# Gate products of the last stage as two 64-row halves of TensorE's array, added when PSUM is read

## Chip, cores and metric

The kernel runs on one NeuronCore of a Trainium2 chip, as one launch. The metric is the device time of that launch in microseconds (us). All inputs and the output lie in HBM, and everything is float32. The profile is of one execution; its trace has every instruction with its start and duration.

## What is computed

The reference is one layer of a hybrid decoder on 512 tokens of 2048 channels. The change lies in its last step, a gated input embedding ahead of the final norm:

```python
n3 = rms_norm(h, norm_ple[i])
h = h + jax.nn.sigmoid(n3 @ w_ple_gate[i]) * (p[i] @ w_ple_proj[i])
return rms_norm(h, norm_final)
```

`n3 @ w_ple_gate` is a product of 512x2048 with 2048x2048. What stands ahead of it (pooling mixer, gated DeltaNet, a mixture of 32 experts) is computed as before, and so is `p @ w_ple_proj`, which is ready when the last stage begins.

## The kernel before

Tokens lie on partitions in NT = 4 groups of P = 128, called t; the 2048 channels that are summed over are KD = 16 groups of 128, called k. Float32 products are made to float32 accuracy from a rounded part (hi, of type float32r) and a rest (lo): `mm3` (line 97) issues hi*hi, hi*lo and lo*hi into one PSUM bank, at lines 99, 100 and 101. Each is a matmul with a weight load of its own. The scheduler of the framework may order the three as it likes.

A PSUM bank holds 128x512 float32. There are eight: `bank("mm")` and `bank("dl")` hand out four each, in turn, and a bank is handed out again once its reader is done.

`last_norm` (four calls, 512 channels each) transposes h and writes it as `xh` and `xl`, 128 channels by 512 tokens for each k. These are the stationary operands of the last stage: 128 channels (the array's rows) by 128 tokens (its columns).

`tail` (line 1532) is the last stage. It walks over the 2048 output channels in five blocks: three of 512, one of 256 (starting at channel 1536) and a last one of 256.

- Blocks 0 to 3 share a loop. For every k and every t one `mm3` adds to the bank of t. The banks of the four t are taken from "mm" in blocks 0 and 2 and from "dl" in blocks 1 and 3.
- `gate_weights` (line 1523) hands out the gate's weights, split into hi (a ScalarE copy, line 94) and lo (a VectorE subtraction, line 95) in pieces of 128x1024, four buffers each.
- After a block `finish` runs for each t: a tanh on ScalarE out of PSUM (line 1549), two operations on VectorE (lines 1551 and 1554), a sum of squares on ScalarE (line 1556) and a product with the final gain on GpSimd (line 1557). Its buffer `th3` exists twice.
- Block 4 goes t by t instead, with one "dl" bank for each, and ends with the final norm of that t and the store.

Two places ahead of the last stage already use parts of TensorE's array. The router (line 919) multiplies with 36 columns of weights and puts the product of k into PSUM partitions from 64 * (k % 2) on, so that even and odd k use different halves of the array's columns. The experts (lines 1138 and 1197) put two experts of 64 slots side by side in the same way, in pairs of matmuls to partitions 0 to 63 and 64 to 127 of one bank. Both use all 128 rows and plain float32, and in the trace a plain float32 product stands as two matmuls.

The order on each engine in this stage is set by the framework's scheduler, not by hand.

Of the kernel before, what the change touches and what calls it, by code (L numbers as in the profile page):

```python
# [13 lines left out]
AF = mybir.ActivationFunctionType  # L14
OP = mybir.AluOpType
# [4 lines left out]
NT = T // P  # L20
D = 2048
KD = D // P
# [40 lines left out]
class Layer:  # L63
# [33 lines left out]
    def mm3(self, ps, whi, wlo, xhi, xlo, start, stop):  # L97
        mm = self.nc.tensor.matmul
        mm(ps, whi, xhi, start=start, stop=False)  # L99
        mm(ps, whi, xlo, start=False, stop=False)  # L100
        mm(ps, wlo, xhi, start=False, stop=stop)  # L101


    def identity(self):
# [1427 lines left out]
    def tail(self, pp):  # L1532
        nc, a, ss, xh, xl = self.nc, self.a, self.ss3, self.xh, self.xl
        gain, _ = self.take("gain", (D,))
        self.fill_stream(1000)
        nc.sync.dma_start(gain, bass.AP(tensor=a["norm_final"].tensor, offset=a["norm_final"].offset,
                                        ap=[[0, P], [1, D]]))
        m = pp.tile([P, NT], F32, name="ms3", bufs=1)
        nc.vector.tensor_reduce(m, ss, axis=AX.X, op=OP.add)
        nc.vector.tensor_scalar(m, m, 1.0 / D, EPS, op0=OP.mult, op1=OP.add)  # L1540
        hr = pp.tile([P, NT], F32, name="hr3", bufs=1)
        self.rsqrt(pp, hr, m, NT)
        nc.vector.tensor_scalar(hr, hr, 0.5, None, op0=OP.mult)
        ss4 = pp.tile([P, NT, 5], F32, name="ss4", bufs=1)

        def finish(t, c0, w, i, ps):
            cs = slice(c0, c0 + w)
            th = pp.tile([P, T], F32, name="th3", bufs=2)
            nc.scalar.activation(th[:, 0:w], ps[:, 0:w], AF.Tanh, scale=hr[:, t:t + 1])
            o = c0 % T  # L1550
            nc.vector.scalar_tensor_tensor(th[:, 0:w], th[:, 0:w], 1.0, self.pj[t, c0 // T][:, o:o + w],
                                           op0=OP.add, op1=OP.mult)
            d = self.h[:, t, cs]
            nc.vector.scalar_tensor_tensor(d, th[:, 0:w], 0.5, d, op0=OP.mult, op1=OP.add)
            j = self.p_sq.tile([P, T], BF16, name="sqj", bufs=1)
            nc.scalar.activation(j[:, 0:w], d, AF.Square, accum_out=ss4[:, t, i:i + 1])
            nc.gpsimd.tensor_tensor(d, d, gain[:, cs], op=OP.mult)

        for i, (c0, w) in enumerate(((0, 512), (512, 512), (1024, 512), (1536, 256))):
            tag = "dl" if i % 2 else "mm"  # L1560
            ps = [self.bank(tag) for _ in range(NT)]
            k = 0
            while k < KD:
                for hi, lo in self.gate_weights(w):
                    for j in range(1024 // w):
                        for t in range(NT):
                            s = slice(t * P, (t + 1) * P)
                            self.mm3(ps[t][:, 0:w], xh[k][:, s], xl[k][:, s], hi[:, j, :], lo[:, j, :],
                                     start=k == 0, stop=k == KD - 1)
                        k += 1  # L1570
            for t in range(NT):
                finish(t, c0, w, i, ps[t])
        c0, w = 1792, 256
        ws = [part for _ in range(2) for part in self.gate_weights(w)]
        for t in range(NT):
            ps = self.bank("dl")
            s = slice(t * P, (t + 1) * P)
            for k in range(KD):
                hi, lo = ws[k // 4]
                self.mm3(ps[:, 0:w], xh[k][:, s], xl[k][:, s], hi[:, k % 4, :], lo[:, k % 4, :],  # L1580
                         start=k == 0, stop=k == KD - 1)
            finish(t, c0, w, 4, ps)
            m = pp.tile([P, 1], F32, name="ms4", bufs=2)
            nc.vector.tensor_reduce(m, ss4[:, t, :], axis=AX.X, op=OP.add)
            nc.vector.tensor_scalar(m, m, 1.0 / D, EPS, op0=OP.mult, op1=OP.add)
            r = pp.tile([P, 1], F32, name="r4", bufs=2)
            self.rsqrt(pp, r, m, 1)
            ht = self.h[:, t, :]
            nc.vector.tensor_scalar(ht[:, 0:D // 2], ht[:, 0:D // 2], r, None, op0=OP.mult)
            nc.scalar.activation(ht[:, D // 2:], ht[:, D // 2:], AF.Copy, scale=r)  # L1590
            nc.sync.dma_start(a["out"][0, t * P:(t + 1) * P, :], ht)
# [115 lines left out]
```

## Time and profile before

| | us |
|---|---|
| median of 2 runs | 2620.73 (2619.27 to 2622.2) |
| the profiled execution's own time | 2616.97 |
| its span, first to last instruction | 2614.9 |
| TensorE (PE) busy | 2511.0, 96% of the span |
| VectorE (DVE) busy | 1148.9 |
| ScalarE (ACT) busy | 776.7 |
| mean granted clock of TensorE | 0.992 of 2.4 GHz |

The profiled execution lies 3.76 us under the median. 2.1 us of its time lie outside the span. The last stage is its last 190 us or so, from 2424 us on. PE counts matmuls and PEld weight loads, which are instructions of their own and may run beside a matmul. A matmul's duration holds the time until its results are written, so that durations of neighbours overlap: what one costs in a row of many is the distance between starts.

### The profile page before, as it was taken

What the parts mean: (1) busy time and instruction counts of PE and PEld (TensorE: products, weight loads), DVE (VectorE), ACT (ScalarE), POOL (GpSimd) and SP (SyncE); (2) the same over time, 40 slices, a digit from 0 to 9 for tenths busy, and PEclk for the clock granted to TensorE, in tenths of its full rate; (3) what the DMA queues carried; (4) which work ended last, traced back from release to release, by engine and by line L of the source; (5) the groups of instructions that cost most, each with busy time, mean ns of one, the idle gap of its engine ahead of it and who ended that gap; (6) DMA issues with size and microseconds to landing.
All of it is one profiled execution on the core that took longest, in us unless ns stands there. A gap on an engine that the chain in (4) does not pass through costs nothing. (4 is left out here: it accounts for less than half of the span.)

```text
span 2614.9 us, 30940 instructions
## 1 busy us (share of the span) xinstructions
PE 2511.0 (96%) x12358; PEld 1720.5 (66%) x12358; DVE 1148.9 (44%) x2042; ACT 776.7 (30%) x1308; POOL 83.8 (3%) x92
## 2 busy tenths in 40 slices
PE   7999999999999999999989899999999999989998
PEld 6788888887888888877754444444444444444788
DVE  6475766765222233345453343333334333315435
ACT  4233242424222222234434222223222222113323
POOL 1001110100000000000000000000000000000001
PEclk9999999999999999999989999999999999999999
DMA  5222223234333333373237799999999999977222
GB/s 153 81 79 73 79 58 94 68 97 125 97 97 97 97 97 97 97 292 126 81 138 283 324 378 416 379 422 374 422 377 421 384 421 376 401 307 278 97 97 97
DMA packets 197975, 554.16 MB, mean 212 GB/s; under 512 B 30378, under 2 KB 127043, under 8 KB 148035
## 3 DMA queue, kind: packets, MB, share of 16 engines
q1 hardware_dynamic: 194610, 543.61, 55.4%
q10 hardware_dynamic: 2640, 4.33, 0.5%
q0 software_dynamic: 576, 4.19, 0.4%
q8 instruction: 99, 1.62, 0.2%
q14 instruction: 50, 0.40, 0.0%
HBM read 545.01 MB, written 7.08 MB: 211 GB/s over the span
## 5 line engine op out<-in xcount | busy, mean ns | idle before, releaser
L1138 PE MATMUL ps_mm<-wm,xe 128*64 128x512 f32 x2048 | 454.7, 597 | 10.6 <-DMA wm<-in_w_gate_dram 5.3
L99 PE MATMUL ps_mm<-n1h,whi 128*128 128x512 f32 x1120 | 450.4, 402 | 0.9 <-ACT whi L94 0.9
L101 PE MATMUL ps_mm<-n1h,wlo 128*128 128x512 f32 x1120 | 437.3, 391 | 1.7 <-DVE wlo L95 1.6
L100 PE MATMUL ps_mm<-n1l,whi 128*128 128x512 f32 x1120 | 437.1, 390 | 0.0
L95 DVE TENSOR_TENSOR wlo<-raw,whi 128x1024 fp32r<-128x1024 f32 x206 | 254.4, 1235 | 412.5 <-ACT whi L94 401.4
L94 ACT CAST whi<-raw 128x1024 fp32r<-128x1024 f32 x206 | 216.3, 1050 | 545.1 <-PE ps_mm L100 538.9
L1138 PEld LDWEIGHTS ps_mm<-wm,xe 128*64 128x64 f32 x2048 | 141.8, 137 | 287.0 <-issue 264.1
L95 DVE TENSOR_TENSOR glo<-h,ghi 128x512 fp32r<-128x512 f32 x128 | 137.2, 1096 | 361.1 <-ACT ghi L94 352.8
L94 ACT CAST ghi<-h 128x512 fp32r<-128x512 f32 x128 | 139.6, 1134 | 425.3 <-PE ps_dl L1113 314.2
L101 PEld LDWEIGHTS ps_mm<-n1h,wlo 128*128 128x128 f32 x1120 | 210.0, 188 | 47.3 <-DVE wlo L95 2.5
L99 PEld LDWEIGHTS ps_mm<-n1h,whi 128*128 128x128 f32 x1120 | 210.8, 188 | 40.3 <-ACT whi L94 1.3
L100 PEld LDWEIGHTS ps_mm<-n1l,whi 128*128 128x128 f32 x1120 | 210.9, 188 | 38.7
L1197 PE MATMUL ps_mm<-wm,hmT 128*64 128x512 f32 x960 | 218.8, 601 | 9.0 <-DVE eidx L1353 6.9
L1221 DVE TENSOR_TENSOR h<-h,ps_dl 128x512 f32<-128x512 f32 x256 | 160.2, 682 | 98.7 <-PE ps_dl L1219 95.9
L1197 PEld LDWEIGHTS ps_mm<-wm,hmT 128*64 128x64 f32 x960 | 66.5, 137 | 135.2 <-issue 130.0
L1113 PE MATMUL ps_dl<-G,ghi 128*128 128x256 f32 x512 | 134.2, 298 | 1.9 <-DVE G L1092 0.9
L1114 PE MATMUL ps_dl<-G,glo 128*128 128x256 f32 x512 | 128.5, 288 | 5.2 <-DVE glo L95 5.2
L1113 PEld LDWEIGHTS ps_dl<-G,ghi 128*128 128x128 f32 x512 | 99.2, 194 | 42.4 <-issue 38.9
L1218 PE MATMUL ps_dl<-yhi,GT 128*128 128x512 f32 x256 | 107.8, 421 | 14.0 <-ACT xe L1120 14.0
L1114 PEld LDWEIGHTS ps_dl<-G,glo 128*128 128x128 f32 x512 | 99.2, 194 | 7.1 <-DVE glo L95 6.9
L101 PE MATMUL ps_mm<-whi,ml 128*128 128x512 f32 x256 | 100.0, 391 | 2.1 <-DVE ml L95 2.1
L1219 PE MATMUL ps_dl<-ylo,GT 128*128 128x512 f32 x256 | 100.7, 393 | 0.0
(402 smaller groups left out, 3262.4 us busy)
## 6 DMA issues: line engine op xcount, KB each, us to landing
wm<-in_w_gate_dram SPq DMA_DIRECT2D x128, 1024.0 KB, 8.7
wm<-in_w_up_dram SPq DMA_DIRECT2D x128, 1024.0 KB, 10.2
wm<-in_w_down_dram SPq DMA_DIRECT2D x128, 1024.0 KB, 9.5
raw<-in_w_in_dram SPq DMA_DIRECT2D x144, 512.0 KB, 3.7
raw<-in_w_out_dram SPq DMA_DIRECT2D x32, 512.0 KB, 3.7
wm<-in_w_ple_gate_dram SPq DMA_DIRECT2D x16, 1024.0 KB, 5.0
raw<-in_w_up_dn_dram SPq DMA_DIRECT2D x16, 512.0 KB, 3.5
raw<-in_w_up_pool_dram SPq DMA_DIRECT2D x16, 512.0 KB, 3.6
```

Of the source, the lines that this page charges most:

```text
L94: i = self.nc.scalar.copy(hi, src)
L95: return i, self.nc.vector.tensor_tensor(lo, src, hi.bitcast(F32), op=OP.subtract)
L99: mm(ps, whi, xhi, start=start, stop=False)
L100: mm(ps, whi, xlo, start=False, stop=False)
L101: mm(ps, wlo, xhi, start=False, stop=stop)
L1113: nc.tensor.matmul(p, hi[:, t, :], Gf[:, t, :], start=t == 0, stop=False)
L1114: nc.tensor.matmul(p, lo[:, t, :], Gf[:, t, :], start=False, stop=t == NT - 1)
L1138: nc.tensor.matmul(ps[64 * i:64 * i + 64, :], xe[k][:, c0 + 64 * i:c0 + 64 * i + 64], ws[i][:, j, :], start=k == 0, stop=k == KD - 1)
L1197: nc.tensor.matmul(out[cb][64 * i:64 * i + 64, :], hT[:, k, 64 * i:64 * i + 64], ws[i][:, cb * T:(cb + 1) * T], start=k == 0, stop=k == 3)
L1218: nc.tensor.matmul(pc, GT[:, s], yh, start=True, stop=False)
L1219: nc.tensor.matmul(pc, GT[:, s], yl, start=False, stop=True)
L1221: nc.vector.tensor_tensor(d, d, pc, op=OP.add)
```

## The change

A new helper `mm3_rows` takes the place of `mm3` in blocks 0 to 3. For each of the three products it issues two matmuls in place of one: the first with the upper 64 rows of both operands, the second with the lower 64. The halves go to two banks, one "mm" and one "dl", so that a block now holds all eight. `finish` begins with a ScalarE copy of the first bank into `th3` and a VectorE addition of the second; the tanh then reads `th3` in place of PSUM. Block 4 is as it was: it hands `finish` a list of one bank.

```diff
+    def mm3_rows(self, ps, whi, wlo, xhi, xlo, start, stop):
+
+        mm = self.nc.tensor.matmul
+        for w, x, first, last in ((whi, xhi, start, False), (whi, xlo, False, False), (wlo, xhi, False, stop)):
+            for i, r in enumerate((slice(0, 64), slice(64, 128))):
+                mm(ps[i], w[r], x[r], start=first, stop=last)
...
         def finish(t, c0, w, i, ps):
             cs = slice(c0, c0 + w)
             th = pp.tile([P, T], F32, name="th3", bufs=2)
-            nc.scalar.activation(th[:, 0:w], ps[:, 0:w], AF.Tanh, scale=hr[:, t:t + 1])
+            if len(ps) == 2:
+                nc.scalar.copy(th[:, 0:w], ps[0][:, 0:w])
+                nc.vector.tensor_tensor(th[:, 0:w], th[:, 0:w], ps[1][:, 0:w], op=OP.add)
+                ps = [th]
+            nc.scalar.activation(th[:, 0:w], ps[0][:, 0:w], AF.Tanh, scale=hr[:, t:t + 1])
...
         for i, (c0, w) in enumerate(((0, 512), (512, 512), (1024, 512), (1536, 256))):
-            tag = "dl" if i % 2 else "mm"
-            ps = [self.bank(tag) for _ in range(NT)]
+            ps = [[self.bank("mm"), self.bank("dl")] for _ in range(NT)]
...
-                            self.mm3(ps[t][:, 0:w], xh[k][:, s], xl[k][:, s], hi[:, j, :], lo[:, j, :],
-                                     start=k == 0, stop=k == KD - 1)
+                            self.mm3_rows([p[:, 0:w] for p in ps[t]], xh[k][:, s], xl[k][:, s], hi[:, j, :],
+                                          lo[:, j, :], start=k == 0, stop=k == KD - 1)
...
-            finish(t, c0, w, 4, ps)
+            finish(t, c0, w, 4, [ps])
```

The scheduler's order moves at the seams between blocks. TensorE where block 0 ends and block 1 begins, before: the banks of block 1 ("dl") are others than those of block 0 ("mm"). In a row stand the output, then the moving operand and the stationary one.

```order
L101 MATMUL ps_mm_17156<-whi_17361,xl_17094 128x512
L99 MATMUL ps_dl_17417<-whi_17423,xh_16908 128x512 [waits Activation_49]
L100 MATMUL ps_dl_17417<-wlo_17424,xh_16908 128x512 [waits DVE_49]
L101 MATMUL ps_dl_17417<-whi_17423,xl_16909 128x512
L99 MATMUL ps_dl_17418<-whi_17423,xh_16908 128x512 [waits PE_49]
```

The same place with the change, from the end of block 0 through t = 0 and the start of t = 1; t = 2 stands like t = 1:

```order
L108 MATMUL ps_dl_17160<-whi_17533,xl_17094 128x512
L108 MATMUL ps_mm_17621<-whi_17631,xh_16908 128x512 [waits Activation_49]
L108 MATMUL ps_dl_17622<-whi_17631,xh_16908 128x512 [waits DVE_49]
L108 MATMUL ps_mm_17621<-wlo_17632,xh_16908 128x512
L108 MATMUL ps_dl_17622<-wlo_17632,xh_16908 128x512
L108 MATMUL ps_mm_17621<-whi_17631,xl_16909 128x512
L108 MATMUL ps_dl_17622<-whi_17631,xl_16909 128x512
L108 MATMUL ps_mm_17623<-whi_17631,xh_16908 128x512 [waits Activation_49]
L108 MATMUL ps_dl_17624<-whi_17631,xh_16908 128x512 [waits DVE_49]
```

The two halves of a product now stand one behind the other, and the first of each t waits for ScalarE and its partner for VectorE. For t = 3 the three of the "mm" bank stand ahead of the three of the "dl" bank.

ScalarE at the same seam, before:

```order
L1549 ACTIVATE th3_17389<-ps_mm_17153,hr3_17138 128x512 [waits PE_49]
L1549 ACTIVATE th3_17396<-ps_mm_17154,hr3_17138 128x512 [waits PE_49]
L94 CAST whi_17509<-wm_17331 128x1024 [waits DVE_49,PE_49]
L1556 ACTIVATE sqj_17393,ss4_17152<-h_8839 128x512 [waits DVE_49]
L1549 ACTIVATE th3_17403<-ps_mm_17155,hr3_17138 128x512
```

And with the change (line 1557 is now the copy, 1560 the tanh, 1567 the sum of squares):

```order
L1557 COPY th3_17585<-ps_mm_17153 128x512 [waits PE_49]
L1560 ACTIVATE th3_17585<-th3_17585,hr3_17138 128x512 [waits DVE_49]
L1557 COPY th3_17594<-ps_mm_17155 128x512 [waits PE_49]
L1560 ACTIVATE th3_17594<-th3_17594,hr3_17138 128x512 [waits DVE_49]
L1567 ACTIVATE sqj_17591,ss4_17152<-h_8839 128x512 [waits DVE_49]
L1557 COPY th3_17603<-ps_mm_17157 128x512 [waits PE_49]
L94 CAST whi_17789<-wm_17479 128x1024 [waits PE_49,Activation_49]
L1567 ACTIVATE sqj_17600,ss4_17152<-h_8839 128x512 [waits DVE_49,Activation_49]
L1560 ACTIVATE th3_17603<-th3_17603,hr3_17138 128x512 [waits DVE_49]
L1557 COPY th3_17612<-ps_mm_17159 128x512
```

The copy that frees the first bank of t = 1 now stands behind the tanh of t = 0, which waits for an addition of VectorE; the copies of t = 2 and t = 3 stand behind sums of squares, a weight split and a tanh.

VectorE there with the change (1558 is the addition, 1562 and 1565 the two operations behind it):

```order
L1558 TENSOR_TENSOR th3_17585<-th3_17585,ps_dl_17154 128x512 [waits PE_49,Activation_49]
L1562 SCALAR_TENSOR_TENSOR th3_17585<-th3_17585,pj_15929 128x512 [waits Activation_49]
L1558 TENSOR_TENSOR th3_17594<-th3_17594,ps_dl_17156 128x512 [waits PE_49,Activation_49]
L1565 SCALAR_TENSOR_TENSOR h_8839<-th3_17585,h_8839 128x512 [waits DVE_49]
L1562 SCALAR_TENSOR_TENSOR th3_17594<-th3_17594,pj_15938 128x512 [waits Activation_49]
L1565 SCALAR_TENSOR_TENSOR h_8839<-th3_17594,h_8839 128x512 [waits DVE_49]
L1558 TENSOR_TENSOR th3_17603<-th3_17603,ps_dl_17158 128x512 [waits PE_49,Activation_49]
L95 TENSOR_TENSOR wlo_17790<-wm_17479,whi_17789 128x1024 [waits Activation_49]
L1562 SCALAR_TENSOR_TENSOR th3_17603<-th3_17603,pj_15987 128x512 [waits Activation_49]
L1558 TENSOR_TENSOR th3_17612<-th3_17612,ps_dl_17160 128x512 [waits DVE_49,PE_49,Activation_49]
```

Before, VectorE had no part in freeing a bank here; now the four additions that free the second banks are spread among the eight operations of `finish` and a weight split.

## Rows read from the trace of the kernel before

**Rows 1.** The page, busy us (share of the span) and instructions of each engine.

```profile
PE 2511.0 (96%) x12358; PEld 1720.5 (66%) x12358; DVE 1148.9 (44%) x2042; ACT 776.7 (30%) x1308; POOL 83.8 (3%) x92
```

**Rows 2.** Windows of blocks 1, 3, 4: us, busy of PE PEld DVE ACT POOL, clock, DMA.

```profile
2469.75:2514.50 44.75, 44.75 (x193) 35.97 (x192) 17.41 (x17) 13.49 (x20) 6.32 (x4) 1.00 0.29 95
...
2559.30:2581.70 22.40, 22.40 (x193) 22.35 (x193) 11.74 (x12) 8.71 (x16) 6.33 (x4) 1.00 0.15 48
2581.70:2614.90 33.20, 22.61 (x194) 22.41 (x193) 19.41 (x69) 11.86 (x28) 6.63 (x8) 0.87 0.31 127
```

**Rows 3.** Timeline inside block 0: start us, duration us, engine, line, operation.

```profile
2435.22 0.39 PE L101 MATMUL ps_mm<-whi,xl 128*128 128x512 f32 x1
2435.22 0.19 PEld L99 LDWEIGHTS ps_mm<-whi,xh 128*128 128x128 f32 x1
2435.45 0.40 PE L99 MATMUL ps_mm<-whi,xh 128*128 128x512 f32 x1
```

**Rows 4.** Timeline inside block 3, products 256 wide.

```profile
2569.97 0.28 PE L100 MATMUL ps_dl<-wlo,xh 128*128 128x256 f32 x1
2569.97 0.19 PEld L101 LDWEIGHTS ps_dl<-whi,xl 128*128 128x128 f32 x1
2570.09 0.28 PE L101 MATMUL ps_dl<-whi,xl 128*128 128x256 f32 x1
```

**Rows 5.** TensorE's timeline at 1192 and 1339 us, router products of 36 columns.

```profile
1192.11 1.05 PE L919 MATMUL ps_dl<-hT,wr 128*36 128x512 f32 x2
...
1339.29 1.06 PE L919 MATMUL ps_dl<-hT,wr 128*36 128x512 f32 x4 [0.80 <-ACT hT L917]
```

**Rows 6.** Timeline of weight loads in an expert stage, products of 64 columns.

```profile
2372.05 0.14 PEld L1197 LDWEIGHTS ps_mm<-wm,hmT 128*64 128x64 f32 x2 [0.29 <-issue]
2372.48 0.14 PEld L1197 LDWEIGHTS ps_mm<-wm,hmT 128*64 128x64 f32 x2 [0.28 <-issue]
```

**Rows 7.** The expert products of line 1197: duration ns min/median/max; a window of them.

```profile
L1197 PE MATMUL ps_mm<-wm,hmT x960: 592/592/1116, 1466.1 to 2378.1; 128*64 128x512 f32 x192
...
2371.57:2378.00 6.43, 6.43 (x30) 2.21 (x32) 1.00 1.05 387
```

**Rows 8.** Timeline at 2412.9 us, a product whose weight load nothing covers.

```profile
2412.89 0.50 PE L1218 MATMUL ps_dl<-yhi,GT 128*128 128x512 f32 x1
2413.23 0.40 PE L1219 MATMUL ps_dl<-ylo,GT 128*128 128x512 f32 x1
...
2412.89 0.19 PEld L1218 LDWEIGHTS ps_dl<-yhi,GT 128*128 128x128 f32 x1 [0.24 <-DVE xl L1516]
```

**Rows 9.** Timeline at the seam of blocks 0 and 1: ScalarE, VectorE, GpSimd.

```profile
2467.85 1.39 ACT L1549 ACTIVATE th<-ps_mm,hr 128x512 f32<-128x512 f32 x2 [2.45 <-PE ps_mm L101]
2469.95 1.05 ACT L94 CAST whi<-wm 128x1024 fp32r<-128x1024 f32 x1 [0.71 <-PE ps_mm L101]
2470.90 0.63 ACT L1556 ACTIVATE sqj<-h 128x512 bf16<-128x512 f32 x1
...
2471.09 1.22 DVE L95 TENSOR_TENSOR wlo<-wm,whi 128x1024 fp32r<-128x1024 f32 x1
2472.23 1.78 DVE L1551 SCALAR_TENSOR_TENSOR th<-th,pj 128x512 f32<-128x512 f32 x1
2475.65 0.68 DVE L1551 SCALAR_TENSOR_TENSOR th<-th,pj 128x512 f32<-128x512 f32 x1
...
2471.70 3.47 POOL L1557 TENSOR_TENSOR h<-h,gain 128x512 f32<-128x512 f32 x2 [1008.11 <-ACT sqj L1556]
```

**Rows 10.** VectorE by line and form, 2400 to 2425 us: busy us, mean ns.

```profile
L1221 DVE TENSOR_TENSOR h<-h,ps_dl 128x512 f32<-128x512 f32 x15 | 9.4, 680 | 2.7 <-PE ps_dl L1219 2.7
```

**Rows 11.** Idle time ahead of block 0, and two windows at a lower clock.

```profile
2424.24 0.50 PE L100 MATMUL ps_mm<-wlo,xh 128*128 128x512 f32 x1 [3.11 <-DVE wlo L95]
...
1346.00:1360.00 14.00, 5.99 (x34) 5.62 (x34) 10.13 (x45) 3.76 (x7) 0.00 (x0) 0.53 0.00 0
...
2425.30:2428.80 3.50, 3.50 (x10) 2.72 (x9) 3.02 (x9) 1.30 (x3) 0.00 (x0) 0.51 0.65 199
```

## The prediction

> **What bounds the kernel now.** The page comes first: TensorE is busy for 96% of the span and no other engine for half of it [rows 1]. The change touches only the last stage, so I read that stage by windows, one for each block. In block 1 TensorE is busy for all 44.75 us, in block 3 for all 22.40 us, with ScalarE and VectorE at half that or less [rows 2]. Until block 4 ends nothing but the rate of the matmuls sets the time; only behind it comes a short chain of norm and store that the change leaves alone.
>
> The rate is read from the timeline, as the distance between starts: 0.23 us for a product of 512 columns [rows 3] and 0.12 us for one of 256 [rows 4]. From the windows it is 44.75 / 192 = 0.233 us and 22.40 / 192 = 0.117 us. At the full 2.4 GHz, 512 columns at one a cycle are 0.213 us, so 0.02 us, 9%, is all that is not streaming. The weight load of the next product begins together with the running product and lasts 0.19 us [rows 3]: it costs next to nothing.
>
> **The change part by part.**
>
> *The products.* Blocks 0 to 2 have 3 x 192 = 576 products of 512 columns, block 3 has 192 of 256. Each becomes two of 64 rows, with as many columns to stream as before: 768 matmuls and 768 weight loads more. If the halves of a pair run side by side, a pair costs what one product did and the term is nothing. If they run one after the other, it is 576 x 0.233 + 192 x 0.117 = 134.2 + 22.5 = 156.7 us.
>
> No row of before shows matmuls of fewer than 128 rows side by side. The nearest show halves of the array's columns. A router product of 36 columns alone (two matmuls in the same half) takes 1.05 us; two products, one in each half (four matmuls), take 1.06 us [rows 5]: the second is free. The expert matmuls last 0.592 us each, but 30 of them pass in 6.43 us, one in 0.214 us, and their weight loads come two at a time, every 0.43 us [rows 6, 7]. So TensorE dispatches to two parts of the array at once, loads weights for both ahead of time, and does so for operands that are float32, over hundreds of pairs. I take the same for rows, and a pair at 0.233 us: the term is 0.
>
> Its bounds within this case: as for the columns, the 0.02 us behind each product may vanish (a pair at 0.214 us: 576 x 0.019 + 192 x 0.0095 = 12.8 us gained); more is excluded, since each half streams all its columns. And the doubled weight loads may queue behind one another. A load that nothing covers puts the next start 0.34 us after the first in place of 0.23 us [rows 8], so it takes 0.11 us. Two are 0.22 us: still under the 0.233 us of a wide pair, but over the 0.117 us of a narrow one, which would cost 192 x 0.103 = 19.8 us in block 3. The column pairs, whose two loads appear together within 0.14 us [rows 6], speak for 0.
>
> The Trainium skill (TensorE: Matmul & The Clock Gate, Part 3, The mechanism) has 4 row tiles of 32 rows and 512 columns at 3.07 times the speed; no run here shows that, and by it the term is 0 as well.
>
> *The seams.* This is where I expect the loss. Before, blocks alternate between four banks and four others, and TensorE goes from one block to the next without a gap [rows 2]. Now each block holds all eight, and its first product of t has to wait until both banks of t are read: one by the ScalarE copy, the other by the VectorE addition. Behind the waiting matmul everything else on TensorE is queued.
>
> I put durations on the two orders shown above, from the moment when t = 0 is done (2467.85 us, the first tanh of before [rows 9]). Block 1 began 1.9 us later, at 2469.75 us [rows 2]. Copy and tanh take 0.69 us (half of the 1.39 us for two [rows 9]), the addition 0.68 us as line 1221, which has the same operands, one in PSUM [rows 10], lines 1551 and 1554 some 0.7 us each where GpSimd is idle, a sum of squares 0.63 us and 0.19 us for its read-out, the split's copy 1.05 us and its subtraction 1.22 us [rows 9].
> - t = 0: copy to 0.7, addition to 1.4. The banks are free before 1.9; no wait.
> - t = 1: its copy stands behind the tanh of t = 0, so it ends at 2.8, its addition at 3.5. TensorE is through with t = 0 at 2.6 and through with t = 1 at 4.2.
> - t = 2: copy at 5.7, behind tanh of t = 1 and a sum of squares; addition at 6.4. TensorE is through with it at 7.1.
> - t = 3: copy at 8.9, behind the split, a sum of squares and the tanh of t = 2; addition at 9.7. Its three "dl" halves stand behind its three "mm" halves, so it is through at 10.4.
>
> Without waits TensorE would be there at 1.9 + 12 x 0.233 = 4.7. The seam costs 5.7 us. From some 5 us on GpSimd multiplies by the gain, and beside it VectorE's operations last 1.78 in place of 0.68 us [rows 9]; one or two of the operations that lead to the additions of t = 2 and t = 3 meet it, so I take 6.5 us. The seam of blocks 1 and 2 is alike; at that of blocks 2 and 3 TensorE's order lets some products of the next k pass in the waits: 6 us. The last seam needs one bank for t = 0 and has it at once. Together 19 us, with bounds of 12 (4 us a seam, if the orders mesh better) and 27 us (9 us, if GpSimd meets every addition).
>
> *The start of block 0.* Four lone "dl" halves wait for the transposes' banks, but TensorE idles there for 3.11 us anyway until a weight split is done [rows 11]. That cover hides four halves of 0.23 us; without it they would cost 0.9 us. I take 0.
>
> *The clock.* One microsecond after that idle stretch the granted clock was 0.51, 1.2 GHz for most of 3.5 us, and 10 products passed in place of 15 [rows 11]: 1.2 us lost. A seam now has waits of 1 to 2.5 us. I take one more such fall, 1 us; the bound is 5 us, if one lasts as long as the 14 us at 0.53 around 1350 us [rows 11], of which TensorE is idle for more than half.
>
> *Copies and additions themselves.* 16 copies and 16 additions, 11 us on each engine, lie on engines that are busy for less than half of a block [rows 2]; except at the seams nobody waits for them.
>
> The sum: 2616.97 + 0 + 19 + 0 + 1 = 2637.0 us for this execution. It lies 3.76 us under the median of before, and the forecast is for a median: **2641 us**, 0.8% more than 2620.73. A measurement of this kernel can tell about 2%, 52 us, from no change, so this is no change. The range of this case: 2620.7 - 12.8 + 12 = 2620 us to 2620.7 + 19.8 + 27 + 5 = 2673 us.
>
> **The rivals.**
>
> *The halves run one after the other.* For it: no row shows row halves together; both write all 128 partitions of PSUM at the same time, where column halves write 64 each; and the operands here are of float32r, those of the column pairs plain float32. Against it: rows 5 to 7. The seams then cost less, some 11 us, since the banks of t = 0 have longer to come free: 2620.7 + 156.7 + 11 = 2788 us, 6.4% slower. The side changes where a pair costs about 0.28 us: 2% less 20 us at the seams leaves 32 us over 672 pairs of full width.
>
> *Row halves side by side, but each weight load exposed.* If only a whole array can be loaded ahead, each half waits 0.11 us for its own load [rows 8]: 768 x 0.11 = 84.5 us, with 18 us at the seams 2723 us, 3.9% slower. For it: the 768 extra loads, and PEld is already busy for 22.35 of 22.40 us in block 3 [rows 2] (by durations that hold latency, though). Against it: the column pairs load ahead.
>
> *The loads were exposed, and halves hide them.* Each half could load while its partner streams, and the 0.11 us would be won back 768 times: 2620.7 - 84.5 + 19 = 2555 us, 2.5% faster. Against it: the loads begin together with a product on the same 128 rows [rows 3], and only 0.02 us is left to win. The Trainium skill (TensorE: Matmul & The Clock Gate, Part 3, What overlaps and what doesn't) has weight loads overlap running matmuls only where their row groups differ, which would give this case. The trace does not agree: 0.23 us between starts, where an exposed load makes it 0.34 us.
>
> That the change does not split at all is no rival: the slices are in the code, and the order shows both banks.
>
> **How the numbers follow.** Side by side with stalled seams 0.73; one after the other 0.15, because what I lean on is columns; loads exposed 0.11; loads won back 0.01. The first case lies within 2% (to 2673 us), the next two are slower, the last faster. The range needs 8 in 10: the first case has 0.73, so I add the exposed loads, and it runs from 2618 to 2730 us. That leaves out the serial case.
>
> **What would show it.** In the profile after: pairs of 64-row matmuls starting together with 0.23 us from pair to pair, and windows of block 1 of about 51 us in place of 44.75 with PE busy for all but 5 to 6 of them. Waits of TensorE on the additions (VectorE) for t = 1 and 2 and on the copy (ScalarE) for t = 3, once a seam. If starts are an even 0.23 us apart, half by half, and the window of block 1 is near 90 us, the serial rival holds; 0.34 us from pair to pair means exposed loads; narrow pairs at 0.22 us in block 3 alone, loads in a queue.

## The result and the profile after

The median went from 2620.73 to 2648.6 us (2647.96 to 2649.24, 2 runs), a ratio of 1.0112 with a 95% interval of [1.0083, 1.0142]: 1.1% slower, within what counts as no change here, and 7.6 us over the forecast. The profiled execution has a span of 2647.1 us, against 2614.9 before, and a mean granted clock of 0.985, against 0.992.

The first two groups of rows answer to [rows 1] and [rows 2]. The engine line of the page:

```profile
PE 2535.1 (96%) x13126; PEld 1735.4 (66%) x13126; DVE 1159.6 (44%) x2058; ACT 784.3 (30%) x1324; POOL 82.4 (3%) x92
```

There are 768 matmuls and 768 weight loads more than in [rows 1], and 16 more operations on VectorE and on ScalarE, as the diff has it. The windows of blocks 0 to 4, with the same columns as [rows 2]:

```profile
2428.74:2474.19 45.45, 45.45 (x376) 36.43 (x378) 14.57 (x24) 11.02 (x14) 0.00 (x0) 0.96 0.36 116
2474.19:2527.00 52.81, 49.55 (x387) 37.76 (x384) 20.74 (x20) 15.55 (x25) 5.83 (x4) 0.94 0.25 81
2527.00:2580.70 53.70, 50.44 (x387) 41.34 (x384) 20.73 (x20) 15.73 (x25) 5.81 (x4) 0.90 0.25 79
2580.70:2613.05 32.35, 28.64 (x387) 27.33 (x385) 15.66 (x17) 11.49 (x22) 5.84 (x4) 0.84 0.11 34
2613.05:2647.10 34.05, 22.88 (x193) 22.67 (x192) 20.09 (x72) 13.15 (x31) 6.72 (x8) 0.90 0.30 124
```

Block 0, which needs twice as many matmuls as before, takes 45.45 us. Before, blocks 0 and 2 were these windows:

```profile
2424.24:2469.75 45.51, 45.51 (x188) 36.47 (x189) 15.03 (x25) 11.07 (x13) 0.00 (x0) 0.96 0.35 116
2514.50:2559.30 44.80, 44.80 (x193) 35.98 (x193) 17.46 (x17) 13.49 (x20) 6.33 (x4) 1.00 0.29 94
```

Block 0 took 45.51 us: the halves cost nothing and gain nothing. Blocks 1 and 3 took 44.75 and 22.40 us in [rows 2]; blocks 1, 2 and 3 now take 8.06, 8.90 and 9.95 us more, together 26.9 us. Block 4, which the change leaves alone, takes 0.85 us more than its 33.20 us; I have no cause for that. The sum over the five blocks is 27.7 us, and the medians differ by 27.9 us. (The span differs by 32.2 us; the other 4.5 us had come before block 0 began, nearly all of it in stages that the change doesn't touch. There the granted clock of this execution is 0.50 from 1554.8 to 1558.2 us and from 2353.5 to 2356.9 us, where that of before has 1.00.)

Where block 0 streams, the timeline (as in [rows 3]) shows the halves side by side:

```profile
2439.89 0.39 PE L108 MATMUL ps_mm<-whi,xh 64*128 64x512 f32 x1
2439.89 0.39 PE L108 MATMUL ps_dl<-whi,xh 64*128 64x512 f32 x1
2439.89 0.18 PEld L108 LDWEIGHTS ps_mm<-wlo,xh 64*128 64x128 f32 x1
2439.90 0.18 PEld L108 LDWEIGHTS ps_dl<-wlo,xh 64*128 64x128 f32 x1
2440.12 0.39 PE L108 MATMUL ps_mm<-wlo,xh 64*128 64x512 f32 x1
```

Both halves of a pair start in the same hundredth of a microsecond, the loads for the next pair start with them, and the next pair follows after 0.23 us. In block 3, where a pair has only 0.117 us, two rows of the "dl" half and a load of the "mm" half between them:

```profile
2604.91 0.28 PE L108 MATMUL ps_dl<-whi,xh 64*128 64x256 f32 x1
2604.93 0.19 PEld L108 LDWEIGHTS ps_mm<-wlo,xh 64*128 64x128 f32 x1
...
2605.03 0.27 PE L108 MATMUL ps_dl<-wlo,xh 64*128 64x256 f32 x1
```

0.12 us from pair to pair, as in [rows 4]. A load lasts longer than that and still holds nobody up.

The seam between blocks 0 and 1, TensorE's timeline (the bracket is the idle time ahead and what ended it):

```profile
2474.19 0.39 PE L108 MATMUL ps_mm<-whi,xh 64*128 64x512 f32 x1
...
2475.73 0.50 PE L108 MATMUL ps_dl<-whi,xh 64*128 64x512 f32 x1 [0.36 <-DVE th L1558]
...
2477.57 0.49 PE L108 MATMUL ps_mm<-whi,xh 64*128 64x512 f32 x1 [0.87 <-ACT th L1557]
2479.61 0.63 PE L108 MATMUL ps_dl<-whi,xh 64*128 64x512 f32 x1 [1.55 <-DVE th L1558]
2479.61 0.64 PE L108 MATMUL ps_mm<-wlo,xh 64*128 64x512 f32 x1
...
2480.90 0.79 PE L108 MATMUL ps_mm<-whi,xh 64*128 64x512 f32 x1
2481.49 0.62 PE L108 MATMUL ps_mm<-wlo,xh 64*128 64x512 f32 x1
...
2483.03 0.79 PE L108 MATMUL ps_dl<-whi,xh 64*128 64x512 f32 x1 [0.48 <-DVE th L1558]
2483.04 0.79 PE L108 MATMUL ps_mm<-whi,xh 64*128 64x512 f32 x1
```

Four waits: for the addition of t = 1, the copy and the addition of t = 2, the addition of t = 3. The idle times understate them, since one half runs alone while the other waits. What counts is when TensorE comes to the second k (the last row): 2483.04 us, where 2474.19 + 12 x 0.233 = 2476.99 us would have been in step, so 6.05 us late. And from the third of these waits on, starts are 0.4 to 0.6 us apart, not 0.23: the clock has fallen.

VectorE and ScalarE there, the operations that TensorE waits for and what holds them up:

```profile
2472.29 0.59 ACT L1557 COPY th<-ps_mm 128x512 f32<-128x512 f32 x1 [2.44 <-PE ps_dl L108]
...
2476.95 0.56 ACT L1557 COPY th<-ps_mm 128x512 f32<-128x512 f32 x1
2477.13 1.27 POOL L1568 TENSOR_TENSOR h<-h,gain 128x512 f32<-128x512 f32 x1 [1013.00 <-ACT sqj L1567]
2477.19 1.76 DVE L1565 SCALAR_TENSOR_TENSOR h<-th,h 128x512 f32<-128x512 f32 x1
2478.88 0.68 DVE L1558 TENSOR_TENSOR th<-th,ps_dl 128x512 f32<-128x512 f32 x1
...
2479.85 1.98 POOL L1568 TENSOR_TENSOR h<-h,gain 128x512 f32<-128x512 f32 x1 [1.45 <-ACT sqj L1567]
2480.61 1.77 DVE L1562 SCALAR_TENSOR_TENSOR th<-th,pj 128x512 f32<-128x512 f32 x1
2482.30 0.68 DVE L1558 TENSOR_TENSOR th<-th,ps_dl 128x512 f32<-128x512 f32 x1
```

The additions of t = 2 and t = 3 end 7.3 and 10.7 us after the first copy began; each stands behind an operation that lasts 1.76 or 1.77 us beside GpSimd. At the next seam TensorE comes to the second k at:

```profile
2536.07 0.79 PE L108 MATMUL ps_mm<-whi,xh 64*128 64x512 f32 x1
```

That is 6.27 us late (2527.00 + 2.80 = 2529.80). The stretches at a low clock, as windows:

```profile
2479.80:2486.60 6.80, 6.32 (x24) 4.18 (x24) 6.28 (x6) 2.64 (x6) 3.26 (x2) 0.50 0.50 154
2531.00:2541.30 10.30, 8.28 (x33) 5.90 (x34) 8.11 (x8) 4.41 (x10) 4.77 (x4) 0.50 0.30 102
2585.60:2595.90 10.30, 8.81 (x78) 8.52 (x80) 7.27 (x8) 3.91 (x9) 4.56 (x3) 0.50 0.34 103
```

One behind each seam at 0.50, the lower level of 1.2 GHz. Before, blocks 1, 2 and 3 had 1.00 ([rows 2] and the window above).

### The profile page after: what moved, and what is told of

The parts are those of the page before. It is cut to its first block, busy times and chain, and to the rows that moved or that the text cites. A ratio compares the mean times of both kernels' runs of the same rounds, so it can differ in the third digit from the quotient of the medians.

```text
span 2647.1 us, 32517 instructions
## 1 busy us (share of the span) xinstructions
PE 2535.1 (96%) x13126; PEld 1735.4 (66%) x13126; DVE 1159.6 (44%) x2058; ACT 784.3 (30%) x1324; POOL 82.4 (3%) x92
## 3 DMA queue, kind: packets, MB, share of 16 engines
q10 hardware_dynamic: 2640, 4.33, 0.5%
## 5 line engine op out<-in xcount | busy, mean ns | idle before, releaser
L1145 PE MATMUL ps_mm<-wm,xe 128*64 128x512 f32 x2048 | 457.6, 600 | 10.6 <-DMA wm<-in_w_gate_dram 5.3
L108 PE MATMUL ps_dl<-whi,xh 64*128 64x512 f32 (+1 forms) x256 | 98.3, 384 | 7.8 <-DVE th L1558 7.2
```

What stands on the lines that cost most here:

```text
L108: mm(ps[i], w[r], x[r], start=first, stop=last)
L1145: nc.tensor.matmul(ps[64 * i:64 * i + 64, :], xe[k][:, c0 + 64 * i:c0 + 64 * i + 64], ws[i][:, j, :], start=k == 0, stop=k == KD - 1)
```

## The experiments

Three theories to begin with. A: the loss is the waits at the three seams, because a block holds all eight banks, and the falls of the clock that follow. B: matmuls of 64 rows cost something themselves, or bring the clock down. C: copies and additions are the cost, wherever they stand. After the first runs A became D, below.

| run | median us | ratio to before | 95% interval |
|---|---|---|---|
| e1 full rows, two banks | 2618.35 | 0.9995 | [0.9986, 1.0004] |
| e2 copy and add only | 2618.82 | 1.0 | [0.9991, 1.0009] |
| e3 halves, reads first | 2619.22 | 1.0003 | [0.9994, 1.0012] |
| e4 the same, by scheduler | 2631.87 | 1.0044 | [1.0029, 1.006] |
| e5 halves, t by t at seams | 2622.16 | 1.0008 | [0.9999, 1.0017] |
| e6 full rows, k by k | 2630.82 | 1.0044 | [1.0031, 1.0058] |
| e7 halves, three and three | 2643.07 | 1.0091 | [1.0075, 1.0106] |
| e8 four th3 buffers | 2626.34 | 1.0026 | [1.0015, 1.0036] |
| e9 halves, k by k held | 2649.33 | 1.0118 | [1.0101, 1.0135] |
| e10 waits filled with zeros | 2641.66 | 1.0091 | [1.0075, 1.0108] |
| e11 halves, twelve and twelve | 2638.36 | 1.0072 | [1.0055, 1.0089] |

Before, run beside them: 2618.97 us (e1 to e4), 2620.22 us (e5 to e8), 2619.74 us (e9 to e11).

**e1, e2: full rows.** e1 keeps two banks a t, the copy and the addition, but multiplies with all 128 rows:

```diff
+        mm(ps[0], whi, xhi, start=start, stop=stop)
+        mm(ps[1], whi, xlo, start=start, stop=False)
+        mm(ps[1], wlo, xhi, start=False, stop=stop)
```

> All 128 rows in every matmul again, as before the change, but a product's first matmul goes to the mm bank of its t and the other two to the dl bank, so that each block holds all eight banks and finish copies and adds as in the change. Theory A (the loss is the waits at the three seams, since all banks are held, with the clock falls behind them): the loss stays without any half, some 2640 to 2652 us, windows of blocks 1 and 2 of 51 to 54 us, clock at half for 5 to 10 us behind each seam. Theory B (half-row matmuls cost the time, or thin matmuls bring the clock down): back to 2619 to 2626 us, or seams that wait but no clock falls. Theory C (the copies and additions themselves cost): as theory A here.

It lost nothing, which contradicts theory A as I had put it: all eight banks were held, and copies and additions stood at the seams. A window of its trace, from the first copy of block 0 on and as long as block 1, shows neither a wait nor a fall, and 0.232 us a product (the 45 us behind it are the same):

```profile
2468.17:2513.00 44.83, 44.83 (x193) 35.82 (x192) 18.25 (x20) 15.96 (x24) 6.52 (x4) 1.00 0.28 94
```

The reason stands in the order of TensorE. This is its second seam, and the first has the same order (hi*hi rows of the first 17; 17705, 17707 and 17709 are the "mm" banks of t = 0, 1 and 2):

```
L106 MATMUL ps_mm_17705<-whi_17715,xh_16908 128x512
...
L106 MATMUL ps_mm_17707<-whi_17715,xh_16908 128x512
...
L106 MATMUL ps_mm_17705<-whi_17715,xh_16908 128x512
...
L106 MATMUL ps_mm_17707<-whi_17715,xh_16908 128x512
...
L106 MATMUL ps_mm_17705<-whi_17743,xh_16908 128x512
L106 MATMUL ps_mm_17709<-whi_17715,xh_16908 128x512 x2
```

The scheduler went on with the second k of t = 0 and 1, and began the third of t = 0, before it touched t = 2. With the change it did not: t = 0 to 3 stand one behind the other. Why it orders the halves so differently I did not find out.

e2 keeps the products and banks of before and adds a copy and an addition to `finish` (it adds the one bank to itself and halves the tanh's scale).

> The kernel before (full rows, one bank for each t, four and four banks in turn) with a ScalarE copy and a VectorE addition put into finish for blocks 0 to 3; the addition takes the same bank again and the tanh has half the scale, so that the output is the same. Theory A: nobody waits for them, 2619 to 2624 us. Theory C: the loss is here, some 2640 to 2650 us.

2618.82 us: theory C falls.

**e3, e4: halves, banks read first.** Four buffers `th3`, and all copies and additions written ahead of the rest:

```diff
+                th = pp.tile([P, T], F32, name="th3", bufs=4)
+                read = (nc.scalar.copy(th[:, 0:w], ps[t][0][:, 0:w]),
+                        nc.vector.tensor_tensor(th[:, 0:w], th[:, 0:w], ps[t][1][:, 0:w], op=OP.add))
...
+            with self.behind(read):
+                for t in range(NT):
+                    finish(t, c0, w, i, [ths[t]])
```

e4 is the same without `behind`, so that the scheduler may put operations of `finish` between the reads.

> The change with four th3 buffers, and the copies and additions of all four t put ahead of the rest of finish on ScalarE and VectorE. Theory A: by the durations of the trace the four additions end 1.3, 2.0, 2.7 and 3.4 us after the first copy begins, each ahead of TensorE's need (1.9, 2.6, 3.3, 4.0), so that no seam waits and the clock does not fall: 2617 to 2626 us with all halves still in place. Theory B: stays at 2640 to 2650 us. If halves were worth something in themselves, under 2615 us.

> As the run with the reads first, but the order is left to the scheduler, which lets the tanh of t = 0 and others in between: additions end at 1.3, 3.5, 4.2 and 6.3 us. Theory A: waits of some 2.3 us a seam, about 7 us in all and, if waits of this length do not bring the clock down, 2624 to 2632 us, between the change and the run with the reads first. Theory B: as the change, 2640 to 2650 us.

e3 gives the whole loss back with every half-row matmul in place: theory B falls, and so does any gain from halves. A window as long as block 1 was, from the first seam on: TensorE is busy throughout at 1.00 and passes 193 pairs, as it passed 193 products before [rows 2] (the 44.80 us behind it are the same).

```profile
2473.85:2518.60 44.75, 44.75 (x386) 35.91 (x384) 21.51 (x21) 15.73 (x25) 7.08 (x4) 1.00 0.29 95
```

e4 lies between. Its list of waits between 2432 and 2610 us (total, times, longest) has short waits for the additions and one for a weight split ahead of block 4:

```profile
PE ps_dl L108 <- DVE th L1581: 3.3, 6, 0.8
PE ps_dl L100 <- DVE wlo L95: 2.3, 1, 2.3
```

The granted clock is 0.50 from 2569.9 to 2573.3 us, behind the third seam, and from 2600.6 to 2604.0 us, behind the wait for the weight split. So a part of its 12.9 us belongs to that split and not to the banks.

**Theory D.** The loss needs two things at once: a block that holds all banks, and an order on TensorE that has nothing else to do while they are read. The falls of the clock follow from the waits. That an order k by k alone does no harm the kernel before and e2 show, which have it with four other banks free at each seam. Theory D says that full rows lose too if their order is taken away (e6), and that the change loses nothing if TensorE's order alone is mended (e5).

e5 takes the first four k (eight in block 3) of blocks 1 to 3 t by t, with everything else as in the change; e6 is e1 held to k by k there:

```diff
+                steps = [(q, t) for t in range(NT) for q in ks] if i and k == 0 else [(q, t) for q in ks for t in range(NT)]
+                with self.tc.manual_schedule(engines={mybir.EngineType.PE}) if i and k == 0 else ExitStack():
+                    for q, t in steps:
```

> The change's halves, its two banks and its own finish (two buffers th3, same order of copies, tanh and additions on ScalarE and VectorE), but TensorE takes the first four k of blocks 1 to 3 (eight in block 3) t by t instead of k by k, so that t = 0 and t = 1 fill 5.6 us while the banks of t = 2 and 3 are read. Theory D (the loss needs both: all eight banks held, and a TensorE order that has nothing else to do at the seam; the clock falls only follow from the waits): in the timeline of the change t = 2 comes free 7.3 us and t = 3 10.7 us after the block's last product; this order needs them at 7.5 and 10.3 us, so a wait of some 0.4 us a seam is left: 2618 to 2624 us, clock at its upper level behind the seams. Rival (the additions and copies at the seams slow the matmuls beside them, or bring the clock down themselves): 2635 us or more, since they stand as in the change.

> Full rows into two banks as in the first experiment, but TensorE is held to the written order, k by k and t by t, in the first four k of blocks 1 to 3. No half-row matmul is left. Theory D: with the copies and additions where they stood in the first experiment, t = 2 comes free 5.4 and 6.45 us (its two banks) and t = 3 7.15 us after the block's last product, where TensorE wants them at 3.3 and 4.0 us: 3.2 us of waits a seam, 9.6 us in all, and with a fall of the clock behind some of them 2628 to 2640 us. Rival (the loss belongs to the halves, and full rows on two banks are free in any order): 2617 to 2620 us.

Both came as theory D has it. e5, on the change's own copies and additions, is at 2622.16 us, and its granted clock is 1.00 in all of the stretch that holds the three seams:

```profile
2468.00:2600.00 132.00, 131.72 (x1313) 113.15 (x1310) 70.80 (x99) 51.65 (x93) 22.95 (x18) 1.00 0.25 81
```

e6 loses 10.6 us with full rows. The trace that was kept is of a run of 2623.32 us; the other four took 2629.84 to 2632.41 us at a lower mean clock (0.989 or 0.990 for 0.993), so it shows the least of the loss. Its waits, and its one stretch at a low clock, behind the seam with the longest wait:

```profile
PE ps_mm L106 <- ACT th L1557: 5.0, 3, 2.1
PE ps_dl L107 <- DVE th L1558: 2.0, 3, 0.7
```

```profile
2563.70:2567.20 3.50, 3.37 (x15) 3.37 (x16) 3.40 (x5) 1.50 (x3) 1.85 (x2) 0.51 0.80 244
```

So the clock falls without any half-row matmul too.

**e8: a smaller dose.** The change with `bufs=4` in place of `bufs=2` for `th3`, nothing else.

> The change with four buffers th3 in place of two and nothing else. With them the scheduler puts the copy of t = 2 ahead of the tanh of t = 1, and the addition of t = 3 ahead of the second operation of t = 1. Theory D: by the durations of the change's seam the banks come free 1.3, 3.3, 4.7 and 6.1 us after the block's last product, TensorE is through with t = 3 at 6.8 in place of 4.7 us: waits of 0.7 us three times a seam, 2.1 us, so 6 us in all, and a smaller fall of the clock than in the change, if any: 2624 to 2635 us. If the waits are not what sets the loss, it stays within 2 us of the change's 2648.6 us.

2626.34 us, with waits for the additions of 3.0 us in nine pieces (0.6 the longest) and no fall: 1.00 in the window that holds the seams.

```profile
2470.00:2600.00 130.00, 125.88 (x1235) 104.95 (x1232) 61.17 (x76) 48.20 (x87) 23.91 (x17) 1.00 0.23 74
```

Two more buffers take back over three quarters of the loss: with two, the copy of t = 2 cannot start before t = 0 is done with its buffer; with four it follows the copy of t = 1 at once, so that the order of ScalarE moves with the buffers.

**e9, e10: what the clock costs.** e9 is the change with TensorE held to k by k, the control. e10 adds products with a stationary operand of zeros where TensorE would wait:

```diff
+                        if i and k + q == 0 and t < 3:
+                            for _ in range((3, 14, 11)[t] * 512 // w):
+                                nc.tensor.matmul(ps[0][0][:, 0:w], zero, hi[:, 0, :], start=False, stop=False)
```

> The change with TensorE held to the written order (k by k, t by t, halves alternating) in the first four k of blocks 1 to 3; it is the control for the next run. The copies and additions stand as in the change, so t = 1, 2 and 3 come free 3.4, 7.3 and 10.7 us after the last product of a block and TensorE is through with t = 3 some 6.5 us late, 19.5 us in three seams; the clock falls behind them as in the change. 2640 to 2652 us.

> The control plus products with a stationary operand of zeros, which add nothing, into the first bank of t = 0 while TensorE would wait: 3, 14 and 11 of 0.233 us (twice as many of 256 columns at the last seam) ahead of t = 1, 2 and 3, 6.5 us a seam. The output is the same. Theory D with the clock as a follower (the clock falls because TensorE waits and then runs lone halves at the seam; the waits cost 19 to 20 us, the falls the other 7): no fall behind the seams, and the time is that of the waits alone, 2636 to 2642 us, under the control by some 7 us although it does 84 wide products more. Rival (the falls come from half-row matmuls or from what ScalarE, VectorE and GpSimd do beside them): falls as in the control, 2645 us or more.

e9 came to 29.6 us over before, e10 to 21.9: it does 112 products more (28 at each of two seams, 56 narrow ones at the third) and is 7.7 us faster by the medians of four runs each (2645.18 to 2650.49 us against 2640.99 to 2644.88 us). e9's trace has the clock at 0.50 behind each seam, for 6.8, 10.2 and 6.8 us; the second of these, then two rows of e10's timeline and the window of its first seam and the block behind it:

```profile
2527.60:2537.80 10.20, 7.67 (x32) 5.53 (x34) 7.66 (x8) 3.97 (x10) 4.54 (x3) 0.50 0.31 103
```

```profile
2471.75 3.53 PE L1590 MATMUL ps_mm<-whi,zero 128*128 128x512 f32 x14
...
2478.87 0.50 PE L108 MATMUL ps_mm<-whi,xh 64*128 64x512 f32 x1
```

```profile
2469.10:2521.00 51.90, 51.90 (x410) 40.18 (x410) 20.70 (x20) 15.28 (x24) 5.88 (x4) 1.00 0.26 82
```

No fall, there or at the two seams behind it, so it was TensorE's waiting (and the lone halves that it ran meanwhile) that brought the clock down, not the other engines' work. What the falls cost is less sure. The filling is up to 0.9 us a seam too long: e10 begins t = 3 at 2478.87, 11.6 us after its first copy (2467.25 us), where in the change t = 3 had both banks after 10.7 us. So e10 gives back less than the falls cost: 7.7 us by the medians. But in the two kept traces the time from block 0's first full pair to the end is 218.5 us (e9) and 215.3 us (e10), 3.2 us apart; with three times 0.9 us that makes some 6 us.

**e7, e11: how halves find their partner.** e7 writes the three matmuls of the upper rows of a t ahead of the three of the lower rows; e11 is e5 with twelve ahead of twelve (24 and 24 in block 3) in the first k of blocks 1 to 3.

```diff
-        for w, x, first, last in ((whi, xhi, start, False), (whi, xlo, False, False), (wlo, xhi, False, stop)):
-            for i, r in enumerate((slice(0, 64), slice(64, 128))):
+        for i, r in enumerate((slice(0, 64), slice(64, 128))):
+            for w, x, first, last in ((whi, xhi, start, False), (whi, xlo, False, False), (wlo, xhi, False, stop)):
```

> The change, but for each k and t the three matmuls of the upper rows stand ahead of the three of the lower rows, in place of alternating. If TensorE starts matmuls strictly in order and each half of the rows streams one at a time, the first of the lower three can start beside the last of the upper three and no other pair overlaps: four times 0.233 us in place of three for each k and t, 156.7 / 3 = 52 us more than the change, about 2700 us (2690 to 2710). If TensorE looked past a waiting matmul to the other half, it would stay at 2640 to 2655 us; if halves only overlap in dispatch and not in streaming, 2800 us.

> The order t by t of the earlier run (which came to 2622 us), but in these first four k of blocks 1 to 3 all twelve matmuls of the upper rows of a t stand ahead of the twelve of the lower rows (24 and 24 in block 3). It asks how far TensorE looks past matmuls that wait for the other half of the rows; in groups of three it lost nothing. If it sees only some three ahead, each change of halves leaves 6 of 12 (18 of 24 in block 3) without a partner: 1.4 us for each t in blocks 1 and 2 and 2.1 us in block 3, 19.6 us in all, about 2640 us. If each half has a queue of twelve or more, nothing is lost: 2620 to 2626 us. The start of the first lower matmul in the timeline gives the number.

I expected strict order of starts for e7 and 2700 us; it was wrong. At 2643.07 us e7 loses no more than the change. Its halves run 0.02 us apart at the old pace:

```profile
2440.21 0.39 PE L108 MATMUL ps_mm<-whi,xh 64*128 64x512 f32 x1
2440.23 0.39 PE L108 MATMUL ps_dl<-whi,xh 64*128 64x512 f32 x1
2440.44 0.39 PE L108 MATMUL ps_mm<-wlo,xh 64*128 64x512 f32 x1
```

The "dl" row stands third behind the "mm" row in the program, and starts ahead of the next "mm". e11, where the lower rows stand twelve behind, shows how far that goes. Its first t behind the seam has the upper rows in "mm", from the ninth on:

```profile
2476.57 0.39 PE L1586 MATMUL ps_mm<-whi,xl 64*128 64x512 f32 x1
2476.57 0.50 PE L1586 MATMUL ps_dl<-whi,xh 64*128 64x512 f32 x1
2476.80 0.39 PE L1586 MATMUL ps_mm<-whi,xh 64*128 64x512 f32 x1
...
2477.03 0.39 PE L1586 MATMUL ps_mm<-wlo,xh 64*128 64x512 f32 x1
...
2477.27 0.39 PE L1586 MATMUL ps_mm<-whi,xl 64*128 64x512 f32 x1
```

The first lower matmul starts with the ninth upper one, while three upper ones that stand ahead of it have yet to start; the addition that it waits for had ended at 2474.1 us. At the next two changes of halves (2478.55 and 2480.53 us) it is the ninth again. So here a matmul passes three that wait for the other half of the rows, and no more: 2638.36 us, where 2640 was worked out for three and 2622 for twelve.

## Why the prediction came out

**The products, term 0: right.** Column pairs had been the only evidence, and rows behave alike: 0.233 us a pair, block 0 at 45.45 us against 45.51, and e3 equal to before. Of the bounds, neither the gain of 12.8 us nor the queue of narrow loads (19.8 us) showed.

**The start of block 0: right.** Its four lone halves lie in the wait for the weight split.

**Copies and additions in themselves, 0: right** (e2).

**The seams, 19 us: right in size and in mechanism.** TensorE was 6.05 and 6.27 us late at the second k of blocks 1 and 2, where the prediction took 6.5 (with as much for the third seam, some 18.5 us for 19). The window of block 1 was foreseen at about 51 us and is 52.81, the rest being the clock. The additions of t = 2 and 3 came 0.9 and 1.0 us later than in the sketch (7.3 and 10.7 us for 6.4 and 9.7), because both met GpSimd, for which the prediction had added 0.8 us a seam. It named the copy of t = 3 as a wait; it was the copy of t = 2. But the reason given was half of it. That "each block holds all eight" is not enough, as e1 shows; it takes also the order k by k, which the prediction had before it in the listing and treated as given. e5 and e6 show that this order decides, with halves and without.

**The clock, 1 us with a bound of 5: this step failed.** It took one short fall for the whole stage; there was one behind every seam, of 6.8 and twice 10.3 us at half speed. What is left of blocks 1 and 2 once the lateness is taken off is 8.06 - 6.05 = 2.0 and 8.90 - 6.27 = 2.6 us, about half of the low stretch that remained after TensorE had come to the second k (3.6 and 5.2 us). Block 3 has no such single point, since products of later k pass in its waits; with a lateness like the others', which is assumed, it would have some 3.7 us (39 pairs passed in its low stretch, about 0.21 us apart in place of 0.117, which is 3.6 us). That is about 8 us, over the bound of 5; e10 against e9 says 6 to 8. Less the 1 us forecast it is most of the 7.6 us by which the time lies over the forecast; the 0.85 us of block 4 is another part. The time is in the range all the same, because the bound of the seams, 27 us, left room for it.

**The rivals.** Halves in series, exposed loads and loads won back are all excluded by 0.233 us a pair. One reading of the prediction does not hold: the Trainium skill's 3.07 (TensorE: Matmul & The Clock Gate, Part 3, where it stands under Measured speedup vs the span model) is for four tiles. Four at 3.07 times the speed take 1.3 times as long as one (an estimate from that page's figure), so by it a split product would cost more and not the same. The 0.233 us a pair show no such cost for two halves.

The Trainium skill (TensorE: Matmul & The Clock Gate, Part 3, What overlaps and what doesn't) has matmuls start and end strictly in program order. The trace of e11 does not agree: the lower matmul that starts at 2476.57 us stands behind the upper one of 2477.27 us in the program, and ends at 2477.07, before that one starts. By that rule e7 would have come to about 2700 us, as its expectation works out; it came to 2643.07.

## What to carry to other kernels

Splitting a product that fills the array's rows gained nothing here, where its loads were already hidden, and it doubles the banks that a block holds; before giving a stage all of PSUM, check whether TensorE's order has other work for the time in which the banks are read, and mend that order, the order of the reads, or the number of buffers behind them first. Price waits of TensorE at their own length plus the stretch at half clock that may follow: here it was 6.8 to 10.3 us behind each seam, some 6 to 8 us in all beside 18 to 19 us of waits.

## What the runs showed of the hardware

- Two matmuls of 64 rows of float32r, each to all 128 columns and its own PSUM bank, run side by side at full rate: 0.233 us a pair of 512 columns, 0.117 us of 256, with 0.18 to 0.19 us weight loads of both hidden.
- The 0.02 us that each product takes beyond its columns (0.233 us against 0.213 us for 512 of them at one a cycle of 2.4 GHz) stays when it is split: a pair takes 0.233 us.
- TensorE starts a matmul ahead of up to three earlier ones that wait for the other half of the rows (e7, e11). A matmul that waits for a semaphore lets nobody pass: at the seams of the change the second matmul of the "mm" half starts only with its waiting partner (2479.61 us).
- Zero products in the waits kept the granted clock at 1.00 where it fell to 0.50 without them (e10 against e9: 7.7 us by the medians, 3.2 us by the kept traces).
